# A row-wise log-sum-exp: in-place exp in a 48-row ring, shrinking loads, two-operand row sums, and a range check with a second branch

## The chip, the cores and the metric

The kernel runs on one NeuronCore of one Trainium2 chip. The metric is the device time of one execution in microseconds. ACT is the engine of the activation functions, DVE the vector engine, PE the matrix engine, POOL and SP the two others; SP issues the loads here. Every transfer runs on the core's 16 DMA engines.

## The reference

```python
x = randn(32, 512, 1024).astype(float32)
max_x = np.max(x, axis=-1, keepdims=True)
out = max_x.squeeze(-1) + np.log(np.sum(np.exp(x - max_x), axis=-1))
```

There are 16,384 rows of 1,024 numbers, 67.1 MB to read, and one float32 result per row, 64 KB to write.

## The kernel before

The rows are laid on 128 partitions: partition p holds rows 128 p to 128 p + 127 of the input, so that each partition has 128 rows ("row" below means one such row on all 128 partitions: 128 x 1024 numbers, 0.5 MB), and a load of s rows reads s x 4 KB in one piece per partition. No maximum is subtracted: exp is taken of x itself, summed and logged.

A table `schedule` sets the sizes of the loads: 28 loads of 4 rows, 3 of 2 rows, 10 of 1 row, all issued by SP in this order (L55). A pool of 7 buffers (`xt`) lets SP run ahead; a load waits until ACT has read the buffer that it reuses. ACT takes exp of a whole load into an f16 tile `et` (L66), of which there are 4, and DVE sums that tile along its rows into `sumexp` (L69). Five entries of the table, loads 7, 15 and 21 and the last two, are marked S: there ACT does each row by itself and keeps the row's sum in its accumulator (L59), which a second instruction reads out, and DVE has nothing to do.

After row 115 is put in the program ACT's log of the first 104 sums (L74). SP stores these at the end of its queue (L78); ACT logs the last 24 sums (L80) and stores them itself (L83). Exp and log use different tables on ACT, so the build puts in a table load at each switch: before the first exp, before L74, after it (L66), and before L80.

The tile framework sets the semaphores: each engine works through its own queue in order, and an instruction waits where the tile that it reads or overwrites is still in use.

Of the kernel before, what the change touches and what calls it, by code (L numbers as in the profile page):

```python
# [1 line left out]

# [4 lines left out]


@with_exitstack
def kernel(  # L10
    ctx: ExitStack,
    tc: tile.TileContext,
    x: bass.AP,
    out: bass.AP,
):
    nc = tc.nc
    P = nc.NUM_PARTITIONS
    fp32 = mybir.dt.float32
    f16 = mybir.dt.float16
    AF = mybir.ActivationFunctionType  # L20
    AX = mybir.AxisListType

    x_flat = x.flatten_outer_dims()
    n, d = x_flat.shape
    assert n % P == 0
    NC = n // P

    x_rows = x_flat.rearrange("(p c) d -> p c d", p=P)
    out_view = out.rearrange("a b -> (a b)").rearrange("(p c) -> p c", p=P)

    schedule = []
    for i in range(28):
        schedule.append((4, "S" if i in (7, 15, 21) else "V"))
    schedule += [(2, "V")] * 3
    schedule += [(1, "V")] * 8
    schedule += [(1, "S")] * 2
    assert sum(s for s, _ in schedule) == NC

    RMAX = max(s for s, _ in schedule)

    BULK_END = 104
    BULK_LN_AFTER_C0 = 114

    data = ctx.enter_context(tc.tile_pool(name="data", bufs=7))
    scratch = ctx.enter_context(tc.tile_pool(name="scratch", bufs=4))
    stats = ctx.enter_context(tc.tile_pool(name="stats", bufs=1))
    outp = ctx.enter_context(tc.tile_pool(name="outp", bufs=1))

    sumexp = stats.tile([P, NC], fp32)
    res = outp.tile([P, NC], fp32)  # L50

    c0 = 0
    for size, style in schedule:
        xt = data.tile([P, RMAX, d], fp32)
        nc.sync.dma_start(out=xt[:, 0:size, :], in_=x_rows[:, c0 : c0 + size, :])  # L55
        et = scratch.tile([P, RMAX, d], f16)
        if style == "S":
            for r in range(size):
                nc.scalar.activation(  # L59
                    out=et[:, r, :],  # L60
                    in_=xt[:, r, :],
                    func=AF.Exp,
                    accum_out=sumexp[:, c0 + r : c0 + r + 1],
                )
        else:
            nc.scalar.activation(  # L66
                out=et[:, 0:size, :], in_=xt[:, 0:size, :], func=AF.Exp
            )
            nc.vector.reduce_sum(  # L69
                out=sumexp[:, c0 : c0 + size], in_=et[:, 0:size, :], axis=AX.X  # L70
            )
        c0 += size
        if c0 == BULK_LN_AFTER_C0 + 2:
            nc.scalar.activation(  # L74
                out=res[:, 0:BULK_END], in_=sumexp[:, 0:BULK_END], func=AF.Ln
            )

    nc.sync.dma_start(out=out_view[:, 0:BULK_END], in_=res[:, 0:BULK_END])  # L78

    nc.scalar.activation(  # L80
        out=res[:, BULK_END:NC], in_=sumexp[:, BULK_END:NC], func=AF.Ln
    )
    nc.scalar.dma_start(out=out_view[:, BULK_END:NC], in_=res[:, BULK_END:NC])  # L83


# [1 line left out]
_INS = ['x']  # L87
_OUTS = [((32, 512), 'float32')]


# [23 lines left out]
```

## Time and profile before

| | us |
|---|---|
| time, median of 3 executions | 172.71 (172.23 to 173.03) |
| span of the profiled execution, first to last instruction | 170.0 |
| DVE busy in it | 126.1 |
| ACT busy in it | 124.9 |
| loads: 67.1 MB, mean over the span | 395 GB/s |

The profile is of one execution. Its time as a whole is not given beside its span; the median time lies 2.7 us over the span. The slices show in tenths how busy an engine was in each fortieth of the span. The stretches give, for a window of time, its length, the busy time of DVE, ACT and POOL with their numbers of instructions, the clock, the busy share of the DMA engines and the GB/s moved. The chain lists, from the last instruction backwards, what each step had to wait for, as start, duration and name; a name that ends in q is an engine's queue. In the groups stand the engine, the operation, the result and the operand with their shapes, the count, then busy time in us and the mean of one in ns, then the idle time in front and what ended it.

### The profile page before, as it was taken

The page shows a single profiled execution, that of the slowest core. Times are in us where ns is not written, and L with a number is a line of the kernel's source. Part 1 is how long each engine was busy: PE and PEld are TensorE (multiplying, and loading weights), DVE is VectorE, ACT ScalarE, POOL GpSimd, SP SyncE. Part 2 cuts the span into 40 slices and gives each one's busy share as a digit, 9 for nine tenths or more (in the row PEclk, how much of TensorE's full clock was granted, in tenths as well). Part 3 has the DMA queues.
Part 4 walks back from the last instruction along what each step waited for, and adds up shares of the span by engine and source line. Part 5 has one row for each costly group of instructions (what it writes and reads, how often), then busy time and mean ns, then how long its engine had stood idle before and what let it go on. Part 6 is the DMA issues. An engine that isn't in the chain of part 4 may idle for free.

```text
span 170.0 us, 266 instructions
## 1 busy us (share of the span) xinstructions
DVE 126.1 (74%) x36; ACT 124.9 (73%) x70; POOL 0.2 (0%) x4
## 2 busy tenths in 40 slices
DVE  0028998888709888888907888880798888699990
ACT  3078766676987667678887667887777699994973
POOL 0000000000000000000000000000000000000000
DMA  5999999999999999999999999999999999999600
GB/s 197 432 432 432 432 432 428 428 432 424 432 428 432 432 432 428 420 432 428 432 420 420 432 432 428 432 432 422 428 432 428 432 411 422 406 412 406 253 0 3
DMA packets 6194, 67.19 MB, mean 395 GB/s; under 512 B 944, under 2 KB 944, under 8 KB 2224
## 3 DMA queue, kind: packets, MB, share of 16 engines
q1 hardware_dynamic: 6048, 67.16, 93.7%
q10 hardware_dynamic: 144, 0.01, 0.1%
q14 instruction: 2, 0.02, 0.0%
HBM read 67.11 MB, written 0.07 MB: 395 GB/s over the span
## 4 chain that ended last, share of the span: by engine, by line
DMA 71%; ACT 13%; DVE 11%; SPq 1%; DVEq 1%; issue 0%; ACTq 0%
DMA xt<-in_x_dram 71%; DVE sumexp L69 11%; ACT et L66 11%; SPq L55 1%; ACT L80 1%; ACT L66 1%; ACT L74 1%; DVEq L109 1%; ACT res L74 0%; ACT res L80 0%; ACTq L66 0%; ACTq L80 0%
## 5 line engine op out<-in xcount | busy, mean ns | idle before, releaser
L69 DVE TENSOR_REDUCE sumexp<-et 128x4 f32<-128x4096 f16 (+2 forms) x36 | 126.1, 3529 | 39.9 <-ACT et L66 39.9
L66 ACT ACTIVATE et<-xt 128x4096 f16<-128x4096 f32 (+2 forms) x36 | 104.2, 2904 | 36.8 <-DMA xt<-in_x_dram 33.9
L59 ACT ACTIVATE et<-xt 128x1024 f16<-128x1024 f32 x14 | 14.6, 1045 | 3.9 <-DMA xt<-in_x_dram 3.8
L66 ACT ACT_TABLE_LOAD x2 | 2.6, 1283 | 0.7 <-PEq L98 0.7
L59 ACT ACTIVATION_READ_ACCUMULATOR et<-xt 128x1 f32 x14 | 2.6, 186 | 0.0
L80 ACT ACT_TABLE_LOAD x1 | 1.3, 1283 | 1.1 <-DVE sumexp L69 1.1
L74 ACT ACT_TABLE_LOAD x1 | 1.3, 1283 | 0.0
L74 ACT ACTIVATE res<-sumexp 128x104 f32<-128x104 f32 x1 | 0.3, 289 | 0.0
L80 ACT ACTIVATE res<-sumexp 128x24 f32<-128x24 f32 x1 | 0.2, 222 | 0.0
L98 POOL MEMSET const-bfloat16-1.0<- 128x1 bf16 x1 | 0.1, 103 | 0.0
L98 POOL MEMSET const-uint8-127<- 128x1 uint8 x1 | 0.1, 103 | 0.0
L98 POOL MEMSET const-float32-1.0<- 128x1 f32 x1 | 0.1, 100 | 0.0
L98 POOL MEMSET const-float32-0.0<- 128x1 f32 x1 | 0.1, 99 | 0.2 <-issue 0.2
## 6 DMA issues: line engine op xcount, KB each, us to landing
xt<-in_x_dram SPq DMA_DIRECT2D x28, 2048.0 KB, 30.6
xt<-in_x_dram SPq DMA_DIRECT2D x10, 512.0 KB, 6.5
xt<-in_x_dram SPq DMA_DIRECT2D x3, 1024.0 KB, 25.6
out_dram<-res SPq DMA_DIRECT2D x1, 52.0 KB, 4.9
out_dram<-res ACTq DMA_DIRECT2D x1, 12.0 KB, 1.4
```

The lines of the kernel that those rows point to most:

```text
L55: nc.sync.dma_start(out=xt[:, 0:size, :], in_=x_rows[:, c0 : c0 + size, :])
L59: nc.scalar.activation(out=et[:, r, :], in_=xt[:, r, :], func=AF.Exp, accum_out=sumexp[:, c0 + r : c0 + r + 1],)
L66: nc.scalar.activation(out=et[:, 0:size, :], in_=xt[:, 0:size, :], func=AF.Exp)
L69: nc.vector.reduce_sum(out=sumexp[:, c0 : c0 + size], in_=et[:, 0:size, :], axis=AX.X)
L74: nc.scalar.activation(out=res[:, 0:BULK_END], in_=sumexp[:, 0:BULK_END], func=AF.Ln)
L80: nc.scalar.activation(out=res[:, BULK_END:NC], in_=sumexp[:, BULK_END:NC], func=AF.Ln)
L98: nc = _bacc.Bacc("TRN2", target_bir_lowering=False, num_devices=1)
L109: with _tile.TileContext(nc) as tc:
```

## The change

The pools give way to one tile `ring` of 48 rows (fp32, 192 KB per partition). Seventeen loads of 16, 16, 16, 16, 13, 10, 9, 7, 6, 5, 4, 3, 2, 2, 1, 1 and 1 rows fill it in turn (L76); row c lies at place c mod 48, and a load waits until the rows that it overwrites have been used. ACT takes exp of up to four rows at a time in place, in fp32 (L87). DVE then sums each row with one two-operand instruction (L90): it adds the first half of the row, 512 elements, to the second, writes the result over the first half, and puts the accumulated sum into `sumexp`. The last five rows are accumulated on ACT (L80). One table set that has exp and log is loaded at the start (L57).

After row 113 stand ACT's log of the first 112 sums (L96) and a range check of them; after the last row, the log of the last 16 (L102), one store of all results on SP (L103), and the check of these 16. A check clamps the sums to 1e-15 to 1e15 (L62), compares the clamped with the plain ones and adds up the differences (L66), and a matmul with ones adds this up over the partitions in PSUM (L70). DVE turns the count into an integer (L105), all five engines load it into a register (L107), compare and branch (L111). If any sum is out of range, a second pass with subtracted maxima does all rows again; with the input given here none is, and the branch is not entered.

```diff
-    for i in range(28):
-        schedule.append((4, "S" if i in (7, 15, 21) else "V"))
...
+    RING = 48
+    loads = [16, 16, 16, 16, 13, 10, 9, 7, 6, 5, 4, 3, 2, 2, 1, 1, 1]
+    ACCUMULATED_FROM = NC - 5
+    FIRST_CHECK = 112
...
+    nc.scalar.preload_act_table_set("natural_log_exp_and_others")
+    nc.vector.memset(ones, 1.0)
...
+    def check(c0, c1, i, last):
+        nc.vector.tensor_scalar(
+            out=clamped[:, c0:c1], in0=sumexp[:, c0:c1],
+            scalar1=LOW, scalar2=HIGH, op0=ALU.max, op1=ALU.min,
+        )
+        nc.vector.scalar_tensor_tensor(
+            out=clamped[:, c0:c1], in0=clamped[:, c0:c1], scalar=0.0, in1=sumexp[:, c0:c1],
+            op0=ALU.bypass, op1=ALU.not_equal, accum_out=bad[:, i : i + 1],
+        )
+        nc.tensor.matmul(count, lhsT=bad[:, i : i + 1], rhs=ones, start=i == 0, stop=last)
...
-    for size, style in schedule:
-        xt = data.tile([P, RMAX, d], fp32)
-        nc.sync.dma_start(out=xt[:, 0:size, :], in_=x_rows[:, c0 : c0 + size, :])
-        et = scratch.tile([P, RMAX, d], f16)
...
+    for size in loads:
+        p0 = c0 % RING
+        assert p0 + size <= RING
+        nc.sync.dma_start(out=ring[:, p0 : p0 + size, :], in_=x_rows[:, c0 : c0 + size, :])
+        if c0 >= ACCUMULATED_FROM:
...
+        else:
+            for b in range(0, size, 4):
+                s = min(4, size - b)
+                v = ring[:, p0 + b : p0 + b + s, :]
+                nc.scalar.activation(out=v, in_=v, func=AF.Exp)
+                for r in range(b, b + s):
+                    lo = ring[:, p0 + r, 0:H]
+                    nc.vector.scalar_tensor_tensor(
+                        out=lo, in0=lo, scalar=1.0, in1=ring[:, p0 + r, H:d],
+                        op0=ALU.mult, op1=ALU.add,
+                        accum_out=sumexp[:, c0 + r : c0 + r + 1],
+                    )
+        if c0 < FIRST_CHECK <= c0 + size:
+            nc.scalar.activation(
+                out=res[:, 0:FIRST_CHECK], in_=sumexp[:, 0:FIRST_CHECK], func=AF.Ln
+            )
+            check(0, FIRST_CHECK, 0, False)
+        c0 += size
...
+    nc.scalar.activation(out=res[:, FIRST_CHECK:NC], in_=sumexp[:, FIRST_CHECK:NC], func=AF.Ln)
+    nc.sync.dma_start(out=out_view, in_=res)
+    check(FIRST_CHECK, NC, 1, True)
+    nc.vector.tensor_copy(out=nbad, in_=count)
+
+    outside = nc.values_load(
+        nbad[0:1, 0:1], min_val=0, max_val=P * NC, 
+        skip_runtime_bounds_check_because="a count of sums"
+    )
+    with tc.If(outside > 0):
...
```

The order of the instructions on three engines, as the built programs have it, at the places that matter below. In brackets stand the engines and DMA semaphores that an instruction waits for; a count behind a row means as many equal instructions. First ACT before, at its end:

```order
L59 ACTIVATE et,sumexp<-xt 128x1024 [waits DMAHW7_49,DVE_49]
L59 ACTIVATE et,sumexp<-xt 128x1024 [waits DMAHW0_49,DVE_49]
L80 ACT_TABLE_LOAD [waits DVE_49]
L80 ACTIVATE res<-sumexp 128x24 [waits Activation_49]
L83 DMA out_dram<-res 128x24 [waits Activation_49]
```

The last table load and log stand behind DVE's last sum. ACT now, from the last row that comes before the first log to the branch:

```order
L87 ACTIVATE ring<-ring 128x1024 [waits DVE_49]
L96 ACTIVATE res<-sumexp 128x112 [waits DVE_49]
L87 ACTIVATE ring<-ring 128x4096 [waits DMAHW2_49,Activation_49]
L87 ACTIVATE ring<-ring 128x3072 [waits DMAHW3_49,Activation_49]
L87 ACTIVATE ring<-ring 128x2048 [waits DMAHW4_49]
L80 ACTIVATE ring,sumexp<-ring 128x1024 [waits DMAHW5_49]
L80 ACTIVATE ring,sumexp<-ring 128x1024 [waits Activation_49]
L80 ACTIVATE ring,sumexp<-ring 128x1024 [waits DMAHW6_49,Activation_49]
L80 ACTIVATE ring,sumexp<-ring 128x1024 [waits DMAHW7_49]
L80 ACTIVATE ring,sumexp<-ring 128x1024 [waits DMAHW0_49]
L102 ACTIVATE res<-sumexp 128x16 [waits DVE_49,Activation_49]
L107 TENSOR_LOAD nbad [waits DVE_49]
```

The first log (L96) waits for DVE and stands ahead of fourteen rows' exp; the table loads are gone. Next the whole of DVE before:

```order
L109 UNCONDITIONAL_BRANCH [waits barrier_Pool_Activation_PE_DVE_SP_release]
L69 TENSOR_REDUCE sumexp<-et 128x4 [waits Activation_49] x25
L69 TENSOR_REDUCE sumexp<-et 128x2 [waits Activation_49] x3
L69 TENSOR_REDUCE sumexp<-et 128x1 [waits Activation_49] x8
L109 UNCONDITIONAL_BRANCH
```

And DVE now, from the sum of row 113 to the branch:

```order
L90 SCALAR_TENSOR_TENSOR ring,sumexp<-ring 128x512 [waits Activation_49]
L62 TENSOR_SCALAR clamped<-sumexp 128x112 [waits DVE_49]
L66 SCALAR_TENSOR_TENSOR clamped,bad<-clamped,sumexp 128x112 [waits DVE_49]
L90 SCALAR_TENSOR_TENSOR ring,sumexp<-ring 128x512 [waits Activation_49]
L90 SCALAR_TENSOR_TENSOR ring,sumexp<-ring 128x512 x3
L90 SCALAR_TENSOR_TENSOR ring,sumexp<-ring 128x512 [waits Activation_49]
L90 SCALAR_TENSOR_TENSOR ring,sumexp<-ring 128x512 x2
L90 SCALAR_TENSOR_TENSOR ring,sumexp<-ring 128x512 [waits Activation_49]
L90 SCALAR_TENSOR_TENSOR ring,sumexp<-ring 128x512
L62 TENSOR_SCALAR clamped<-sumexp 128x16 [waits DVE_49,Activation_49]
L66 SCALAR_TENSOR_TENSOR clamped,bad<-clamped,sumexp 128x16 [waits DVE_49]
L105 CAST nbad<-count 1x1 [waits PE_49]
```

Row sums are one instruction a row, the first check stands between those of rows 113 and 114, and the second check, the cast and the register load end the queue. Last SP before, at its end:

```order
L55 DMA xt<-in_x_dram 128x1024 [waits DMAHW7_49,Activation_49]
L55 DMA xt<-in_x_dram 128x1024 [waits DMAHW0_49,Activation_49]
L55 DMA xt<-in_x_dram 128x1024 [waits DMAHW1_49,Activation_49]
L78 DMA out_dram<-res 128x104
L109 UNCONDITIONAL_BRANCH
```

And SP now, from the last loads to the branch:

```order
L76 DMA ring<-in_x_dram 128x2048 [waits DMAHW5_49,DVE_49]
L76 DMA ring<-in_x_dram 128x1024 [waits DMAHW6_49,DVE_49]
L76 DMA ring<-in_x_dram 128x1024 [waits DMAHW7_49,DVE_49]
L76 DMA ring<-in_x_dram 128x1024 [waits DMAHW0_49,DVE_49]
L103 DMA out_dram<-res 128x128 [waits DMAHW1_49,Activation_49]
L107 TENSOR_LOAD nbad [waits DVE_49]
L111 COMPARE_AND_BRANCH
```

A load now waits for DVE's sums of the rows that it overwrites, and one store stands where the first of two stood, ahead of the register load.

More of the change, by code (lines that the diff above doesn't have):

```diff
@@ L6 @@
 from concourse._compat import with_exitstack
+LOW, HIGH = 1e-15, 1e15
 @with_exitstack
@@ L18 @@
     fp32 = mybir.dt.float32
-    f16 = mybir.dt.float16
+    i32 = mybir.dt.int32
     AF = mybir.ActivationFunctionType
     AX = mybir.AxisListType
+    ALU = mybir.AluOpType
     x_flat = x.flatten_outer_dims()
@@ L26 @@
     NC = n // P
+    H = d // 2
     x_rows = x_flat.rearrange("(p c) d -> p c d", p=P)
     out_view = out.rearrange("a b -> (a b)").rearrange("(p c) -> p c", p=P)
-    schedule = []
-    for i in range(28):
-        schedule.append((4, "S" if i in (7, 15, 21) else "V"))
[L34 to L42, printed above, removed]
@@ L44 @@
-    data = ctx.enter_context(tc.tile_pool(name="data", bufs=7))
-    scratch = ctx.enter_context(tc.tile_pool(name="scratch", bufs=4))
-    stats = ctx.enter_context(tc.tile_pool(name="stats", bufs=1))
-    outp = ctx.enter_context(tc.tile_pool(name="outp", bufs=1))
-    sumexp = stats.tile([P, NC], fp32)
-    res = outp.tile([P, NC], fp32)
-    c0 = 0
-    for size, style in schedule:
-        xt = data.tile([P, RMAX, d], fp32)
-        nc.sync.dma_start(out=xt[:, 0:size, :], in_=x_rows[:, c0 : c0 + size, :])
-        et = scratch.tile([P, RMAX, d], f16)
-        if style == "S":
+    RING = 48
@@ new lines @@
+    loads = [16, 16, 16, 16, 13, 10, 9, 7, 6, 5, 4, 3, 2, 2, 1, 1, 1]
+    ACCUMULATED_FROM = NC - 5
+    FIRST_CHECK = 112
+    assert sum(loads) == NC
+    big = ctx.enter_context(tc.tile_pool(name="big", bufs=1))
+    stats = ctx.enter_context(tc.tile_pool(name="stats", bufs=1))
+    psum = ctx.enter_context(tc.tile_pool(name="psum", bufs=1, space=bass.MemoryType.PSUM))
+    ring = big.tile([P, RING, d], fp32, name="ring")
+    sumexp = stats.tile([P, NC], fp32, name="sumexp")
+    res = stats.tile([P, NC], fp32, name="res")
@@ new lines @@
+    clamped = stats.tile([P, NC], fp32, name="clamped")
+    bad = stats.tile([P, 2], fp32, name="bad")
+    ones = stats.tile([P, 1], fp32, name="ones")
+    nbad = stats.tile([1, 1], i32, name="nbad")
+    count = psum.tile([1, 1], fp32, name="count")
+    nc.scalar.preload_act_table_set("natural_log_exp_and_others")
[10 more added lines that the diff above has]
+        nc.tensor.matmul(count, lhsT=bad[:, i : i + 1], rhs=ones, start=i == 0, stop=last)
@@ L58 @@
+    c0 = 0
+    for size in loads:
[3 more added lines that the diff above has]
+        if c0 >= ACCUMULATED_FROM:
             for r in range(size):
+                v = ring[:, p0 + r, :]
                 nc.scalar.activation(
-                    out=et[:, r, :],
-                    in_=xt[:, r, :],
-                    func=AF.Exp,
+                    out=v, in_=v, func=AF.Exp, accum_out=sumexp[:, c0 + r : c0 + r + 1]
+                )
[17 more added lines that the diff above has]
+        c0 += size
@@ new lines @@
+    nc.scalar.activation(out=res[:, FIRST_CHECK:NC], in_=sumexp[:, FIRST_CHECK:NC], func=AF.Ln)
[5 more added lines that the diff above has]
+        skip_runtime_bounds_check_because="a count of sums"
+    )
+    with tc.If(outside > 0):
+        STEP = 8
+        for k, c0 in enumerate(range(0, NC, STEP)):
+            p0 = (k % 2) * STEP
+            xt = ring[:, p0 : p0 + STEP, :]
+            neg = clamped[:, c0 : c0 + STEP]
+            nc.sync.dma_start(out=xt, in_=x_rows[:, c0 : c0 + STEP, :])
+            nc.vector.tensor_reduce(out=neg, in_=xt, op=ALU.max, axis=AX.X, negate=True)
+            for r in range(STEP):
+                v = ring[:, p0 + r, :]
+                nc.scalar.activation(
+                    out=v, in_=v, func=AF.Exp, bias=clamped[:, c0 + r : c0 + r + 1],
@@ L63 @@
                     accum_out=sumexp[:, c0 + r : c0 + r + 1],
                 )
[L65 to L83, printed above, removed]
+        nc.scalar.activation(out=res, in_=sumexp, func=AF.Ln)
+        nc.vector.tensor_sub(out=res, in0=res, in1=clamped)
+        nc.sync.dma_start(out=out_view, in_=res)
 _INS = ['x']
```

## The prediction

> **What bounds the kernel now.** I read the slices of the page first, then the stretches, the chain of waits, the groups by shape, and last the first and the last load in the order of time.
>
> ```profile
> DVE  0028998888709888888907888880798888699990
> ACT  3078766676987667678887667887777699994973
> DMA  5999999999999999999999999999999999999600
> ```
>
> The DMA row is full from the second slice to the 37th; DVE and ACT are not. For most of the span the load stream is the limit. Then it stops, and DVE and ACT work on for two to three slices. The stretches give rates:
>
> ```profile
> 8.00:20.00 12.00, 7.79 (x2) 9.36 (x3) 0.00 (x0) 1.00 1.01 434
> 20.00:140.00 120.00, 94.47 (x23) 90.85 (x47) 0.00 (x0) 1.00 1.01 428
> 150.00:157.00 7.00, 7.00 (x5) 4.39 (x5) 0.00 (x0) 1.00 1.03 410
> 160.00:162.00 2.00, 2.00 (x3) 1.86 (x3) 0.00 (x0) 1.00 0.04 13
> ```
>
> The last column is GB/s: 428 with 4-row loads, 410 with 1-row loads, nothing after 160. DVE is busy for all of 150 to 157. The chain shows the end:
>
> ```profile
> 139.39 1.23 ACT L74
> 140.62 0.07 issue
> 140.69 0.29 ACT res L74
> ...
> 140.99 1.28 ACT L66
> ...
> 145.94 17.76 DVE sumexp L69 x10
> 163.70 1.13 DVEq L109
> 164.82 1.14 DVE sumexp L69
> ...
> 166.03 1.28 ACT L80
> ...
> 167.32 0.22 ACT res L80
> ```
>
> Two table loads and a log hold ACT up at 139.4 to 142.3, and from 145.9 DVE is behind: its reductions, one after the other, end at 165.96. Then come a third table load, the last log, and the store:
>
> ```profile
> 163.73 1.06 ACT L59 ACTIVATE et<-xt 128x1024 f16<-128x1024 f32 x1
> 164.69 0.19 ACT L59 ACTIVATION_READ_ACCUMULATOR et<-xt 128x1 f32 x1
> 167.57 0.37 ACTq L83 DMA_DIRECT2D out_dram<-res  x1
> out_dram<-res ACTq DMA_DIRECT2D x1, 12.0 KB, 1.4
> 8.13 3.62 ACT L66 ACTIVATE et<-xt 128x4096 f16<-128x4096 f32 x1 [6.12 <-DMA xt<-in_x_dram]
> 11.78 4.42 DVE L69 TENSOR_REDUCE sumexp<-et 128x4 f32<-128x4096 f16 x1 [11.78 <-ACT et L66]
> L55 SPq DMA_DIRECT2D xt<-in_x_dram x1: 327/327/327, 155.9 to 155.9; - x1
> DMA to landing us min/median/max: 5.1/5.1/5.1
> ```
>
> The store lands 1.4 us after its issue, at 169.0, and the span ends at 170.0, so 1.0 us closes the program. The last load, issued at 155.9, landed at 161.0. Of the 170.0 us, 9 lie behind the stream. The median time, 172.71, is 2.7 us over this span; I carry these 2.7 us unchanged.
>
> **The load stream.** A 4-row load (2.097 MB) takes 4.90 us at 428 GB/s and a 1-row load (0.524 MB) 1.279 us at 410. With a fixed part a and b per row, a + 4b = 4.90 and a + b = 1.279: b = 1.207, a = 0.072 us. The first load landed by 8.1, so the stream starts as if at 8.1 - 4.9 = 3.2. Check on before: 3.2 + 28 x 4.90 + 3 x 2.486 + 10 x 1.279 = 160.65, measured 161.0; I carry the 0.35. After: 3.2 + 128 x 1.207 + 17 x 0.072 + 0.35 = 159.3, a gain of 1.7 us. The 16-row load shows in no row. Its bounds are 1.225 us a row, as with 4-row loads (last landing 160.4), and 1.207 without the fixed part (158.1). I take the fit, since its b is what the 434 GB/s stretch gives as well (0.524/434 = 1.208).
>
> The ring does not starve the stream: rows 0 to 15 land at 22.9, and four exp of 3.62 and the last four sums free them by 41, while the loads already queued last until 61.4. The waits in front of later loads on SP end likewise over 10 us early.
>
> **ACT and DVE per row.** The groups by shape:
>
> ```profile
> L69 DVE TENSOR_REDUCE sumexp<-et 128x4 f32<-128x4096 f16 x25 | 110.5, 4420 | 39.9 <-ACT et L66 39.9
> L66 ACT ACTIVATE et<-xt 128x4096 f16<-128x4096 f32 x25 | 90.4, 3617 | 33.9 <-DMA xt<-in_x_dram 33.9
> L69 DVE TENSOR_REDUCE sumexp<-et 128x1 f32<-128x1024 f16 x8 | 9.1, 1214 | 0.0
> L66 ACT ACTIVATE et<-xt 128x1024 f16<-128x1024 f32 x8 | 8.4, 1054 | 2.9 <-DVE sumexp L69 2.6
> L66 ACT ACTIVATE et<-xt 128x2048 f16<-128x2048 f32 x3 | 5.5, 1894 | 0.0
> L74 ACT ACTIVATE res<-sumexp 128x104 f32<-128x104 f32 x1 | 0.3, 289 | 0.0
> L80 ACT ACTIVATE res<-sumexp 128x24 f32<-128x24 f32 x1 | 0.2, 222 | 0.0
> ```
>
> Exp in place writes fp32 instead of f16. The two logs, fp32 to fp32, differ by 67 ns for 80 elements, 0.84 ns each; exp into f16 differs by 3617 - 1054 = 2563 ns for 3072, 0.83. So I cost the fp32 write at nothing. A 3-row exp is half way between 1.894 and 3.617: 2.76 us.
>
> The row sum over two 512-element halves has no row. DVE's reduction takes (4420 - 1214)/3072 = 1.044 ns an element and 145 ns besides. At one element pair a cycle that is 0.534 + 0.145 = 0.68 us; reading out the accumulator adds between nothing and ACT's 0.19. Between 0.68 and 0.87 I take 0.78. 123 of them are 96 us against 126.1 before, and a block of four takes 3.1 us against ACT's 3.62, so DVE follows ACT. That cover is gone if a row costs much more (first rival).
>
> **Where ACT gets free.** With one table set, three of the four loads of 1.28 us go: two inside the stream, one on the end's path. By the stream's numbers the load of rows 109 to 113 lands at 3.2 + 114 x 1.207 + 10 x 0.072 + 0.35 = 141.9. ACT does four rows (3.62) and one (1.05), to 146.6. Next in its queue is the first log, which waits for the sum of row 111. DVE starts row 109 at 145.6 and ends 111 at 145.6 + 3 x 0.78 = 147.9. So this moved log adds a wait of 1.3 us on ACT, with all the later exp behind it. After 0.29 of log it is 148.2; the next loads have landed by then or land in time, and ACT runs without a gap: 3.62 + 2.76 + 1.89 + 5 x 1.13 (one accumulated row after the other, the starts in before being 1.13 apart: 162.60 to 163.73) = 13.9. All sums are there at 162.2, 2.9 us after the last landing: ACT, no longer DVE, ends last. Before, the same point is 165.96.
>
> ```profile
> 162.60 1.06 ACT L59 ACTIVATE et<-xt 128x1024 f16<-128x1024 f32 x1
> L59 ACT ACTIVATION_READ_ACCUMULATOR et<-xt 128x1 f32 x14 | 2.6, 186 | 0.0
> L98 POOL MEMSET const-float32-1.0<- 128x1 f32 x1 | 0.1, 100 | 0.0
> L55 SPq EVENT_SEMAPHORE  x34: 17/17/17, 8.1 to 154.1; - x34
> ```
>
> **The closing.** Before, 4.0 us follow the last sum: table load, log, store, 1.0. Afterwards two branches run. Log and store: 0.3 + 1.4, then 1.0, so 2.7. The check: clamp 0.15, compare with its accumulator 0.15 + 0.19, matmul 0.2, cast 0.2, and four hand-overs of about 0.05 (0.03 from ACT's exp to DVE at 11.78, 0.07 from DVE to ACT at 166.03) make 1.1; small instructions here lie between 0.10 (the memset) and 0.22 (the log), and I take the middle. TENSOR_LOAD has no row: between one sequencer step (0.017) and a memory round trip (the store's 1.4), taken as 0.7. The jump over the branch: between nothing and another 1.4, taken as 0.35, with 0.4 for some twenty more semaphore steps on SP at 17 ns. With the closing 1.0 the check's branch is 3.6, longer than the store's. Bounds: 2.7 (the store rules) and 1.1 + 1.4 + 1.4 + 0.4 + 1.0 = 5.3. So the span is 162.2 + 3.6 = 165.8 and the time 165.8 + 2.7 = 168.5, 2.4% below before.
>
> **The rivals.**
>
> *Row sums at half rate (slower).* The two-operand sum reads two fp32 operands and keeps an accumulator, which nothing in before does. If it takes two cycles a pair, one row costs 1.069 + 0.145 = 1.21 us, as the 1024-element reduction (1214 ns), or 1.40 with the read-out. DVE starts at 26.6 (22.9 + 3.7) and hardly rests again: row 111 is summed at 26.6 + 112 x 1.21 = 162.1, and log, ACT's 13.9 and the closing put the span at 180, the time at about 183; with 1.40 at about 204. It decides from about 1.08 us a row: from row 64 on (DVE starts it at 100.5) the shrinking loads leave DVE no rest, and 48 rows x 1.08 end at 152.3, which with 0.3, 13.9 and 3.6 is 170. Speaking for it: both operands and the result are fp32. Against: the f16 reduction already gets no benefit from its narrow input, so one element a cycle is no limit of bytes. Chance 0.13.
>
> [...]
>
> *The check costs more (about no change).* If the register load and each of two jumps, into the untaken side and to the program's end, are round trips of 1.4, the closing is 1.1 + 3 x 1.4 + 0.4 + 1.0 = 6.7, the span 168.9, the time 171.6; a round trip more gives 173. For it: five engines load and jump, and the profile has no such step yet. Against: nothing but small reads is involved. Chance 0.15; of it 0.08 faster, 0.05 within, 0.02 slower.
>
> [...]
>
> *Larger loads stream no faster.* At 1.225 us a row, row 113 lands at 143.2 and ACT ends at 163.5: time 169.8. That is the change not doing one of its parts. Chance 0.10, faster as well.
>
> **How the numbers follow.** My forecast has 0.62. A change under about 0.5%, 0.9 us, can't be told from none here. Faster: 0.62 + 0.08 + 0.10 = 0.80; same 0.05; slower 0.13 + 0.02 = 0.15. The range: low, no fixed cost of loads (0.7 less at row 113), sums at 0.68 (0.3 less) and the store ruling the closing (0.9 less) give 166.6, say 166.4; high, the costly check at 171.6 and a little of the slower stream, 172.0. What is left out is the half-rate sum and the worst of the check, 0.16.
>
> **What would show it.** In the changed profile: the sum's group near 780 ns, with or without a second row for the accumulator; exp of 4096 at 3617; loads landing 19.4 us apart at first and the last at 159.3; ACT without gaps from 148.2 to 162.2, with one wait on DVE ahead of the log; about 3.6 us from the last accumulated row to the end. A sum over 1.08 us, an exp slower in place, or over 7 us of closing would make the prediction wrong.

## The result, and the profile after

The changed kernel takes 168.81 us (168.68 to 169.14, median of 4 executions) against 172.59 of the kernel before on the same chip: a ratio of 0.9776, 95% interval 0.9753 to 0.9799, so 2.2% faster. The forecast was 168.5. The span of the profiled execution is 167.0 us against 170.0. In every execution whose own span is on record, of both kernels, the time lies 1.7 to 1.8 us over the span (2.2 in e7). The profile of the kernel before has no time beside its span of 170.0; with 1.8 us it would be 171.8. The other executions of that kernel have spans from 170.2 us up, 170.9 in the median, so its profile shows a short one. Where less than 1 us matters, the times and their ratios decide, not the spans of single executions.

The slices of the changed kernel:

```profile
DVE  0000005665077712776066746757737393584810
ACT  3000049990899519992599879989597979879980
DMA  7979998999799799989999999999999999999800
```

DVE, which was full in four of its last five slices before, is full in none of its last seven now. ACT works through the end, and the loads stop a little earlier. The groups by shape, with busy time and the mean of one in ns behind the bar:

```profile
L87 ACT ACTIVATE ring<-ring 128x4096 f32<-128x4096 f32 x27 | 95.9, 3607 | 44.2 <-DMA ring<-in_x_dram 42.2 <-DVE ring L90 2.0
L90 DVE SCALAR_TENSOR_TENSOR ring<-ring 128x512 f32<-128x512 f32 x123 | 77.6, 687 | 79.1 <-ACT ring L87 78.9
L90 DVE DVE_READ_ACCUMULATOR ring<-ring 128x1 f32 x123 | 10.0, 81 | 0.0
L80 ACT ACTIVATE ring<-ring 128x1024 f32<-128x1024 f32 x5 | 5.2, 1039 | 0.0
```

The two-operand sum takes 687 ns and its read-out 81, together near the 780 of the forecast. Exp in place costs 3607, as with an f16 result. In order of time, around the first log:

```profile
143.01 4.56 ACT L87 ACTIVATE ring<-ring 128x4096 f32<-128x4096 f32 x2 [0.67 <-DMA ring<-in_x_dram]
146.66 0.69 DVE L90 SCALAR_TENSOR_TENSOR ring<-ring 128x512 f32<-128x512 f32 x1 [2.32 <-ACT ring L87]
147.28 0.08 DVE L90 DVE_READ_ACCUMULATOR ring<-ring 128x1 f32 x1
147.28 0.69 DVE L90 SCALAR_TENSOR_TENSOR ring<-ring 128x512 f32<-128x512 f32 x1
...
148.62 0.30 ACT L96 ACTIVATE res<-sumexp 128x112 f32<-128x112 f32 x1 [1.04 <-DVE ring L90]
148.82 3.60 ACT L87 ACTIVATE ring<-ring 128x4096 f32<-128x4096 f32 x1
```

The sums start 0.62 us apart, because the next one starts before the last one's duration is over and the read-out lies beside it. The log waits 1.04 us for DVE; the forecast had 1.3. ACT's last instructions, then the load issues (line 76, from 130 us on: the last load alone), then what stands at the branch:

```profile
160.94 1.04 ACT L80 ACTIVATE ring<-ring 128x1024 f32<-128x1024 f32 x1
161.88 0.18 ACT L80 ACTIVATION_READ_ACCUMULATOR ring<-ring 128x1 f32 x1
162.10 0.21 ACT L102 ACTIVATE res<-sumexp 128x16 f32<-128x16 f32 x1
```

```profile
L76 SPq DMA_DIRECT2D ring<-in_x_dram x1: 328/328/328, 136.9 to 136.9; - x1
...
DMA to landing us min/median/max: 23.4/23.4/23.4
```

```profile
L111 SPq EVENT_SEMAPHORE  x8: 17/17/17, 163.7 to 164.8; - x8
L111 ACTq COMPARE_BRANCH  x1: 50/50/50, 163.5 to 163.5; - x1
L111 SPq COMPARE_BRANCH  x1: 45/45/45, 163.5 to 163.5; - x1
...
L111 ACTq EVENT_SEMAPHORE  x1: 17/17/17, 166.2 to 166.2; - x1
```

The last load lands at about 160.2, all sums are there at 162.1, and the span ends at 167.0. The last block shows what stretches the end: SP goes on 0.2 us after its branch, ACT only 2.7 us after its own, at 166.2. The waits of SP's queue say the same: at the program's end (line 153) it waited 1.0 us for ACT's first step behind the branch.

```profile
SPq L153 <- ACTq L111: 1.0, 1, 1.0
```

### The profile page after: what moved, and what is told of

Same layout as the page of the kernel before. It is cut to its first block, busy times and chain, and to the rows that moved or that the text cites. A ratio compares the mean times of both kernels' runs of the same rounds, so it can differ in the third digit from the quotient of the medians.

```text
span 167.0 us, 438 instructions
## 1 busy us (share of the span) xinstructions
PE 0.4 (0%) x4; PEld 0.2 (0%) x4; DVE 78.8 (47%) x254; ACT 116.3 (70%) x48; POOL 0.2 (0%) x4
## 4 chain that ended last, share of the span: by engine, by line
DMA 73%; ACT 20%; DVE 3%; issue 1%; SPq 0%; PE 0%; ACTq 0%
DMA ring<-in_x_dram 73%; ACT ring L87 17%; ACT ring L80 3%; DVE ring L90 2%; SPq L76 0%; PE count L70 0%; DVE clamped L66 0%; DVE clamped L62 0%; DVE nbad L105 0%; ACTq L87 0%; ACT res L96 0%
## 5 line engine op out<-in xcount | busy, mean ns | idle before, releaser
L87 ACT ACTIVATE ring<-ring 128x4096 f32<-128x4096 f32 (+3 forms) x35 | 109.4, 3190 | 44.2 <-DMA ring<-in_x_dram 42.2
L90 DVE SCALAR_TENSOR_TENSOR ring<-ring 128x512 f32<-128x512 f32 x123 | 77.6, 687 | 79.1 <-ACT ring L87 78.9
L90 DVE DVE_READ_ACCUMULATOR ring<-ring 128x1 f32 x123 | 10.0, 81 | 0.0
L80 ACT ACTIVATE ring<-ring 128x1024 f32<-128x1024 f32 x5 | 5.2, 1039 | 0.0
L62 DVE TENSOR_SCALAR clamped<-sumexp 128x112 f32<-128x112 f32 (+1 forms) x2 | 0.4, 192 | 3.8 <-ACT ring L80 3.8
L96 ACT ACTIVATE res<-sumexp 128x112 f32<-128x112 f32 x1 | 0.3, 297 | 1.0 <-DVE ring L90 1.0
L80 ACT ACTIVATION_READ_ACCUMULATOR ring<-ring 128x1 f32 x5 | 0.9, 185 | 0.0
L70 PE MATMUL count<-ones,bad 128*1 128x1 f32 x4 | 0.4, 164 | 162.4 <-DVE clamped L66 162.4
L66 DVE SCALAR_TENSOR_TENSOR clamped<-clamped,sumexp 128x112 f32<-128x112 f32 (+1 forms) x2 | 0.5, 226 | 0.1
L70 PEld LDWEIGHTS count<-ones,bad 128*1 128x1 f32 x4 | 0.2, 80 | 162.5 <-DVE clamped L66 162.5
L105 DVE CAST nbad<-count 1x1 int32<-1x1 f32 x1 | 0.1, 145 | 0.3 <-PE count L70 0.3
L102 ACT ACTIVATE res<-sumexp 128x16 f32<-128x16 f32 x1 | 0.2, 215 | 0.0
L66 DVE DVE_READ_ACCUMULATOR clamped<-clamped,sumexp 128x1 f32 x2 | 0.2, 82 | 0.0
```

Of the source, the lines that this page charges most:

```text
L62: nc.vector.tensor_scalar(out=clamped[:, c0:c1], in0=sumexp[:, c0:c1], scalar1=LOW, scalar2=HIGH, op0=ALU.max, op1=ALU.min,)
L66: nc.vector.scalar_tensor_tensor(out=clamped[:, c0:c1], in0=clamped[:, c0:c1], scalar=0.0, in1=sumexp[:, c0:c1], op0=ALU.bypass, op1=ALU.n ...
L70: nc.tensor.matmul(count, lhsT=bad[:, i : i + 1], rhs=ones, start=i == 0, stop=last)
L80: nc.scalar.activation(out=v, in_=v, func=AF.Exp, accum_out=sumexp[:, c0 + r : c0 + r + 1])
L87: nc.scalar.activation(out=v, in_=v, func=AF.Exp)
L90: nc.vector.scalar_tensor_tensor(out=lo, in0=lo, scalar=1.0, in1=ring[:, p0 + r, H:d], op0=ALU.mult, op1=ALU.add, accum_out=sumexp[:, c0 + ...
```

## The experiments

Four theories are tested. *Overlap*: before, DVE's lateness and the table loads held up the same end, so that either edit alone brings most of the gain. *Loads*: the small number of large loads is itself worth something. *Check*: the branch costs about 2 us, of which ACT's jump is one part. *Threshold*: a dearer row sum, from 1.08 us a row on, would have undone all. The rivals stand in the expectations.

**e1: one table set alone**, on the kernel before.

```diff
+    nc.scalar.preload_act_table_set("natural_log_exp_and_others")
     c0 = 0
     for size, style in schedule:
```

> The kernel before, with one table set for exp and log and nothing else. Theory A (two delays overlap: the table loads made DVE late, and DVE's lateness set the end): the exp of rows 108 to 111 starts at its landing, 140.6, instead of 142.3, DVE's chain of sums moves 1.7 us ahead, and the last table load of 1.28 goes: 2.9 us less than before, 169.7. Theory B (the three loads inside the stream were covered, only the last one counts): 1.3 us less, 171.3.

Measured: 169.70 us, ratio 0.9829 (0.9808 to 0.9850), 3.0 us less: as theory A has it. The profiled execution doesn't show all of it. It took 170.37, the longest of the five, and stands beside a short one of before. There the load of rows 108 to 111 landed at 142.1 instead of 140.6, and the chain of that execution starts DVE's last run no sooner than before:

```profile
111.39 30.71 DMA xt<-in_x_dram
...
142.18 3.62 ACT et L67
...
145.83 17.76 DVE sumexp L70 x10
...
165.93 0.22 ACT res L81
```

So the span, 168.6, has the 1.3 us of the last table load alone. That the other 1.7 is DVE's earlier start follows from the times and the working, not from this trace.

**e2: two-operand sums alone**, on the kernel before.

```diff
-            nc.vector.reduce_sum(
-                out=sumexp[:, c0 : c0 + size], in_=et[:, 0:size, :], axis=AX.X
-            )
+            for r in range(size):
+                lo = et[:, r, 0 : d // 2]
+                nc.vector.scalar_tensor_tensor(
+                    out=lo, in0=lo, scalar=1.0, in1=et[:, r, d // 2 : d],
+                    op0=mybir.AluOpType.mult, op1=mybir.AluOpType.add,
+                    accum_out=sumexp[:, c0 + r : c0 + r + 1],
+                )
```

> The kernel before, with one two-operand sum per row (on the f16 tile) in place of the reductions, and nothing else; the three switches of table stay. Theory A: DVE no longer ends last. ACT, held up until 142.3 by the tables, is free for the last row when that lands, at 161.1, and ends it at about 163.2 instead of DVE's 165.96: 2.7 us less, 169.9. Theory B (the sums are hidden beside the stream, the gain came from the loads and the tables): under 1 us less, 171.6 or more.

Measured: 169.33 us, ratio 0.9810 (0.9786 to 0.9834), 3.4 us less: theory A. The end now waits for the stream, no longer for DVE (the chain has start and duration; the last load lands at 161.94):

```profile
154.66 7.28 DMA xt<-in_x_dram
...
162.02 0.07 ACT et L59
...
163.19 1.28 ACT L84
```

The sum costs the same on f16 operands as on fp32 ones:

```profile
L71 DVE SCALAR_TENSOR_TENSOR et<-et 128x512 f16<-128x512 f16 x114 | 72.4, 689 | 88.6 <-ACT et L66 88.6
```

**e3: both**, that is, e1's and e2's edits on the kernel before, with its own pools and loads and no check.

> The kernel before, with both: one table set and two-operand sums, but its own pools and loads, and no range check. Theory A: the stream's last landing, 161.1, sets the end; one row of ACT, log and store follow: 168.5, 4.1 us less than before and as fast as the changed kernel, so that ring and large loads brought nothing on balance. Theory B (ring and large loads bring 1.5 us or more of the gain): 170 or more.

Measured: 168.00 us, ratio 0.9737 (0.9709 to 0.9765), 4.7 us less, where e1's and e2's gains would add up to 6.4: the two overlap. The stream now ends last, as its chain shows (start, duration). The row that lands at 160.82 is the last but one; the last lands at 162.03, just as ACT is done with it:

```profile
153.19 7.62 DMA xt<-in_x_dram
...
160.90 1.15 ACT et L60 x2
...
163.29 0.22 ACT res L85
```

That e3 is 0.8 us faster than the whole change seemed to say that ring and loads bring nothing, but the change also has the check, which e3 lacks.

**e4: the change without the check.** It leaves out the test of the range, with the second pass; so does the kernel before.

```diff
-            check(0, FIRST_CHECK, 0, False)
...
     nc.sync.dma_start(out=out_view, in_=res)
-    check(FIRST_CHECK, NC, 1, True)
-    nc.vector.tensor_copy(out=nbad, in_=count)
...
-    with tc.If(outside > 0):
...
```

> The changed kernel without the two checks, the count, the branch and the second pass: it leaves out the test of the range, and ends with log and store. Theory A (the check's branch ends 2.1 us behind the store's: ACT's jump to the program's end waits 2.7 us): the span ends 1.0 us after the store's landing at 163.9, at 164.9 instead of 167.0; time 166.7. Theory B (the closing waits for the store and costs the same either way): 168.5 to 169.

Measured: 166.90 us, ratio 0.9661 (0.9645 to 0.9678): theory A. The check costs 1.9 us. Against e3, e4 is 1.1 us faster, with intervals that don't meet. The two differ in the ring and the loads and in what goes with them: exp in place in fp32, five rows accumulated on ACT instead of 14, the place of the first log, and one store instead of two. So theory A of e3, that ring and loads bring nothing, falls, but e4 alone doesn't say which of these brings the 1.1 us. The next run tests the loads alone.

**e5: the change with the loads of before.**

```diff
-    loads = [16, 16, 16, 16, 13, 10, 9, 7, 6, 5, 4, 3, 2, 2, 1, 1, 1]
+    loads = [4] * 28 + [2] * 3 + [1] * 10
```

The first log moves with it, from behind row 113 to behind row 111.

> The changed kernel with the sizes of loads of before: 28 of 4 rows, 3 of 2 and 10 of 1 in the same ring. Theory A (the size of the loads hardly counts: ACT ends last by 0.7 us, and small loads land last at 161.1 instead of 160.2): ACT ends the last row at 162.3 instead of 162.07, time 168.8 to 169.2. Theory B (each load has a fixed cost of 0.07 us and 24 more of them stand on the path, as the prediction's sum has it): 170.0 or more.

Measured: 170.00 us, ratio 0.9848 (0.9809 to 0.9888), 1.2 us slower than the change: theory B, at its edge. The chain has the last load landing at 162.35, 2.1 us later than in the changed kernel, and ACT only one row behind it:

```profile
152.28 10.08 DMA ring<-in_x_dram
162.35 0.02 issue
162.37 0.03 ACT ring L80
162.40 0.94 issue
163.34 0.20 ACT ring L80
```

The sum of the prediction has 24 loads fewer at 0.072 us, 1.7 us. The size of the loads is worth 1.1 to 1.2 us (e4 against e3, the change against e5); what else separates e4 from e3 is worth nothing that shows.

**e6 and e7: dearer row sums.** A reduction over fp32 takes the place of the two-operand sum, over blocks of up to four rows (e6) or row by row (e7).

```diff
-                for r in range(b, b + s):
-                    lo = ring[:, p0 + r, 0:H]
-                    nc.vector.scalar_tensor_tensor(
...
+                nc.vector.reduce_sum(out=sumexp[:, c0 + b : c0 + b + s], in_=v, axis=AX.X)
```

> The changed kernel with a reduction over each block of up to four fp32 rows in place of the two-operand sums: 4.42 us for four rows, 1.105 a row, just over the 1.08 at which the prediction lets DVE end last. With that working: DVE runs without rest from row 48 on (started at 84.8), sums row 111 at 155.5, one row more for the block; log, ACT's 13.9 and 6.7 of closing and launch make 177. If the threshold is wrong and DVE follows as long as it is faster than the 1.21 us of a landing row: 170 or less.

> The changed kernel with a reduction over each fp32 row in place of the two-operand sum: 1.214 us a row, the price of the first rival (row sums at half rate) without the read-out. With the rival's working: row 111 is summed at 162.5, and log, ACT's 13.9 and 6.7 of closing and launch make 183.5. If DVE's lateness can be made up by ACT or the stream: 177 or less.

Measured: e6 173.49 us, ratio 1.0049 (1.0028 to 1.0071); e7 177.07 us, ratio 1.0258 (1.0208 to 1.0307). Both are slower than before, e6 by 0.5%, so a dearer sum does undo the gain, but the loss is smaller than was worked out; neither expectation of e6, 177 or 170, was met, and e7 lies at the edge of its second, 177 or less. The stretch from 100 to 157 us of e7 (DVE busy is the third pair of numbers), the chain, and ACT around its first log:

```profile
100.00:157.00 57.00, 0.00 (x0) 0.00 (x0) 57.00 (x51) 45.69 (x17) 0.00 (x0) 1.00 1.00 425
```

```profile
142.48 16.98 DVE sumexp L89 x15
```

```profile
147.12 3.62 ACT L87 ACTIVATE ring<-ring 128x4096 f32<-128x4096 f32 x1 [0.36 <-DVE sumexp L89]
157.24 0.30 ACT L93 ACTIVATE res<-sumexp 128x112 f32<-128x112 f32 x1 [6.51 <-DVE sumexp L89]
```

DVE is busy all through this stretch, as the rival had it. But 15 sums take 16.98 us, 1.13 each instead of the 1.21 of one alone, and the framework put the exp of rows 114 to 117 ahead of the log, so that 3.6 us less of ACT's work lies behind it. The working also had the wrong engine at the end: ACT's 13.9 us behind the first log were to end last, but in both runs DVE does, and the last log waits for it (e6, then e7):

```profile
167.21 0.22 ACT L96 ACTIVATE res<-sumexp 128x16 f32<-128x16 f32 x1 [1.47 <-DVE sumexp L88]
170.14 0.22 ACT L99 ACTIVATE res<-sumexp 128x16 f32<-128x16 f32 x1 [2.96 <-DVE sumexp L89]
```

Four 4-row reductions of e6 run in 17.40 us, 1.09 a row, and give 173.5, a little over the time before. So the threshold, 1.08 for a time equal to before, is about right in size; the path by which the prediction came to it is not what these runs show.

**e8: a shorter second pass.** It isn't entered. Maxima, subtraction and sums are on DVE, one exp per 8 rows on ACT: 17 activations in place of 129.

```diff
-            for r in range(STEP):
-                v = ring[:, p0 + r, :]
-                nc.scalar.activation(
-                    out=v, in_=v, func=AF.Exp, bias=clamped[:, c0 + r : c0 + r + 1],
-                    accum_out=sumexp[:, c0 + r : c0 + r + 1],
-                )
+            nc.vector.tensor_tensor(
+                out=xt, in0=xt, in1=neg.unsqueeze(2).to_broadcast([P, STEP, d]), op=ALU.add
+            )
+            nc.scalar.activation(out=xt, in_=xt, func=AF.Exp)
+            nc.vector.reduce_sum(out=sumexp[:, c0 : c0 + STEP], in_=xt, axis=AX.X)
```

> The changed kernel with another second pass: maxima, subtraction and sums on DVE and one exp per 8 rows on ACT, 17 activations in place of 129; it isn't entered. Theory A (ACT's jump over some 300 instructions waits 2.7 us for its code, and that ends the span): ACT's first step behind the branch comes at 163.7 instead of 166.2, SP's steps then end last at 165.3, span 166.0, time 167.9. Theory B (any taken branch on ACT costs 2.7 us, whatever it jumps over): 168.8, as the changed kernel.

Measured: 167.95 us, ratio 0.9727 (0.9693 to 0.9762), 0.9 us under the change: theory A. At the branch of e8:

```profile
L111 SPq EVENT_SEMAPHORE  x8: 17/17/17, 163.7 to 164.4; - x8
L111 ACTq COMPARE_BRANCH  x1: 45/45/45, 163.5 to 163.5; - x1
...
L111 ACTq EVENT_SEMAPHORE  x1: 17/17/17, 163.7 to 163.7; - x1
```

ACT goes on after 0.2 us instead of 2.7. The same step takes 2.4 to 2.7 us in the traces of all six kernels with the long second pass (the change, e5, e6, e7, e9, e12) and 0.2 in the two with the short one (e8, e10). Nothing that runs has changed, only what is jumped over: on ACT 17 activations in place of 129.

**e9: the first log after row 95.**

```diff
-    FIRST_CHECK = 112
+    FIRST_CHECK = 96
```

> The changed kernel with the first log and check after row 95 instead of row 111, where ACT waits for a load anyway. Theory A (the log's wait for DVE, 1.0 us, and its 0.3 stand on ACT's path to the end): ACT is free for the last row when it lands, at 160.2, and ends it at 161.5 instead of 162.07: 0.6 us less, 168.2. Theory B (ACT makes the wait up before the end, the stream alone sets it): 168.8.

Measured: 168.59 us, ratio 0.9768 (0.9743 to 0.9793). The change itself, run beside it (e12), took 168.70: no difference that can be told. Theory B, though for another reason than it gave. In e9, in order of time:

```profile
156.70 1.06 ACT L80 ACTIVATE ring<-ring 128x1024 f32<-128x1024 f32 x1 [0.36 <-DMA ring<-in_x_dram]
157.66 0.19 ACT L80 ACTIVATION_READ_ACCUMULATOR ring<-ring 128x1 f32 x1
157.75 1.04 ACT L80 ACTIVATE ring<-ring 128x1024 f32<-128x1024 f32 x1
...
160.87 1.04 ACT L80 ACTIVATE ring<-ring 128x1024 f32<-128x1024 f32 x1
161.82 0.18 ACT L80 ACTIVATION_READ_ACCUMULATOR ring<-ring 128x1 f32 x1
```

ACT, no longer held up, now waits for the load of rows 123 and 124, which lands at 156.7, and then has five accumulated rows of 1.04 us to do, until 162.0. That is the bound right behind the log's wait, not the landing of the last row.

**e10: e8's and e9's edits together.**

> The changed kernel with both the log after row 95 and the second pass of 17 activations. If the two gains lie one behind the other on the path (0.6 before the last sum, 0.9 after it): 167.3. If one covers the other: 167.9.

Measured: 167.89 us, ratio 0.9726 (0.9701 to 0.9752), the same as e8: the log's place brings nothing here either.

**e11: e4's and e9's edits together.** It leaves out the test of the range.

> The changed kernel without checks, count, branch and second pass (it leaves out the test of the range, as the kernel before does), and with the first log after row 95: 166.9 less 0.6 is 166.3, the fastest version here. If ACT's wait is made up before the end: 166.9.

Measured: 166.44 us, ratio 0.9642 (0.9618 to 0.9666). The lowest median here, and faster than both kernels; against e4, 166.90, the intervals overlap, so that the 0.5 us is open.

**e12: the change again.**

> The changed kernel as it is, beside the three others on one chip: 168.8.

Measured: 168.70 us, ratio 0.9778 (0.9752 to 0.9804).

## Why the prediction was right, point by point

**The load stream.** The fixed part per load, from two rates, was about right. In the traces' semaphore events the first of the 16 DMA engines was done with the last load at 158.2 to 158.7 us in the nine kernels with 17 loads, and at 159.9 to 160.8 in the five with 41; the sum has 1.7 us between them. In the changed kernel the first engine was done at 158.3 and the last at 160.2, where 159.3 was forecast. The term of 0.35, taken over from before, was too small: in that one execution the last engine was 1.0 us behind the first, here 2.0. The ring starved nothing; the DMA engines' busy share from 20 to 140 us is 0.99.

**Row sums.** The forecast took 0.78 us between 0.68 and 0.87; a sum takes 0.687, sums start 0.62 apart, and three in a row with the read-out took 1.9 instead of 2.3. The 0.68 put an element pair at the 1.044 ns of the reduction's element; less the same 145 ns, the 687 make 1.06 ns a pair. The first rival, half rate, is refuted: its row of 1.21 us came neither on fp32 operands (687 ns) nor on f16 ones (689, e2). The argument against it holds in the runs: a reduction of 1024 elements takes 1214 ns from f16 (before) and 1209 from fp32 (e7). Had a row cost that much, e7 shows the order of the loss: slower by 2.6%, not by the rival's 6%, since back-to-back reductions lie 0.08 us closer than their duration says, and the log was moved as well.

**ACT.** All sums were forecast for 162.2 and came at 162.1. The load of rows 109 to 113 was 1.0 us later than reckoned; DVE's sums were 0.4 faster, and ACT's work from the first log's end on took 13.3 us instead of 13.9, an accumulated row 1.04 us after another instead of the 1.13 seen before. So a miss of 1.0 one way and two of 0.4 and 0.6 the other way cancel; the 162.2 is in part luck. ACT ends last, as forecast. The wait ahead of the log is there, 1.04 us, but it costs nothing: e9 took it away and the load of rows 123 and 124 set the same end. "With all the later exp behind it" was right in the order of the queue and wrong as a price.

**The closing.** This is the mis-sized term: 3.6 us forecast, 4.9 measured (162.1 to 167.0). The check itself was shorter than taken, 0.8 us up to the count instead of 1.1, and the register load 0.47 to 0.54 instead of 0.7. Two terms were too small. SP's semaphore steps, taken as 0.4 for some twenty at 17 ns, take 1.6 us: the first eight alone go from 163.7 to 164.8 in the rows at the branch, since they start 0.05 to 0.24 us apart, with one gap of 0.4. In e8, where ACT doesn't wait, they go from 163.7 to 165.4, and the closing is still 4.0 us (162.1 to 166.2). The jump, taken as 0.35, was 2.7 on ACT. Most of that lies beside SP's steps, so it adds 0.9 (e8). Of the second rival's three long steps one came, one jump on one engine. In the changed kernel ACT jumps over more than 250 instructions, counting the read-outs, and goes on 2.7 us after its branch; in e8 it jumps over some 20 and goes on after 0.2. That it waits for its code, as theory A of e8 has it, is the author's guess and not shown: the trace has instruction packets of 8 KB at 164.65 and 165.22 us, inside the wait, but e8 has two at 164.81 and 165.63 as well, and a packet does not say whose code it brings.

**The launch.** Carried over as 2.7 us, it is 1.8 here (168.81 less 167.0), and 1.7 to 1.8 in the executions of the kernel before as well. The 2.7 set the span of one execution, 170.0, beside the median time of others, whose spans are 170.9 in the median; 0.9 of it is that difference. It fits that the last load landed at 160.9 in this execution, and at 161.9 to 162.3 in e1 to e3, which have the same loads. The closing's 1.3 us too little and this 0.9 too much nearly cancel, so the closeness of 168.5 to 168.8 is in part luck.

**Where the gain is.** In times: 172.7 before; 168.0 with table set and sums (e3); 166.9 with the ring, its large loads and what goes with them (e4); 168.8 with the check. Table set and sums bring 4.7 us, though alone they bring 3.0 and 3.4; the large loads bring 1.1 to 1.2; the check takes 1.9 back, 0.9 of it for ACT's jump.

## What to carry to other kernels

When two edits relieve the same end, time each alone and both together: here 3.0 and 3.4 us made 4.7. Take the time outside the span from an execution that has both: here 2.7 us came from two different ones, and 1.8 was right. Before pricing a wait, ask what ends next if it goes; the log's wait of 1.0 us was covered by the landing of one load and the rows behind it. Code that isn't entered cost 0.9 us here: 168.8 us with 129 activations on ACT in the branch, 167.95 with 17 (e8). So try the rare branch in a short form on the engine that ends last.

## What the runs showed of the hardware that was not expected

- A branch on ACT over more than 250 instructions held it for 2.4 to 2.7 us (six kernels), over some 20 for 0.2 (two).
- SP's semaphore steps, 17 to 28 ns long, start 0.05 to 0.24 us apart, with one gap of 0.4: sixteen took 1.6 us in the changed kernel.
- A packet of 64 KB took 2.418 us (median in the trace), four of 16 KB 4 x 0.613 = 2.452: a packet's fixed part is about 0.01 us by these two ((2.452 - 2.418)/3), an estimate. A load has 128 packets, 8 for each of the 16 DMA engines if they share evenly, so this makes some 0.09 us a load, near the 0.072 of the prediction's fit.
- Of the 16 DMA engines the last finished a load 0.5 to 2.3 us after the first, differently from run to run. In the changed kernel this rose from 1.1 to 2.0 us between 120 and 130 us; at 123.8 the trace has an instruction packet of 8 KB, and at 124.1 a load packet took 1.73 us against a median of 1.06. In e6, without such a packet until 169.5 us, it stayed under 1.0 us and the last load landed at 159.5; but in e1 it rose from 0.6 to 1.5 us by 24.5 us without one. That the instruction packet causes it is not shown.
- DVE's two-operand sum costs the same on f16 and fp32 operands, 689 and 687 ns for 512 pairs.
